# VectorE's order at the seams between Strassen products in a hybrid decoder layer

## The chip, the cores and the metric

The kernel runs on one core of a Trainium2 chip. The metric is the device time of one launch in microseconds (us), the median of the runs shown. A profile is one further execution of the same program.

## The reference

One layer of a decoder trunk is applied to a prompt of 512 tokens and to 8 single-token samples. The large products in it are what the change touches:

```python
h   = modulate(rmsnorm(x, norm1_g), sh1, sc1)
z   = h @ w_in                          # 2048 -> 6144: q, k, v and the RWKV inputs
...                                     # windowed attention and RWKV-7 time mixing on z
x   = x + gt1 * (concat(att, rw) @ w_out)               # 2048 -> 2048
h2  = modulate(rmsnorm(x, norm2_g), sh2, sc2)
gate, up = split(h2 @ w_gu, 2)                          # 2048 -> 2 * 5632
x   = x + gt2 * ((silu(gate) * up) @ w_down)            # 5632 -> 2048
```

## The kernel before

The 520 tokens (528 in the first stage) stand along the free axis, features along the 128 partitions. Every large product is made in pieces of 256 output columns by `product` and `combine`, which carry out one level of Strassen's scheme in the Strassen-Winograd form.

`product` goes over pairs of 128-row blocks of the contraction, numbered i from 0: eight of them in the gate, up, output and input products, five or six in the down products. For two pairs at a time it

- loads the weights into a `raw` tile (L130, one DMA for each pair, issued by SyncE). There are two `raw` buffers (`RAW=2`), each for two pairs;
- makes the three weight sums on VectorE (L143, L144, L145), called *weight steps* below;
- for each pair casts the seven weight blocks to their high part on ScalarE (L149) and subtracts to get the *low part* on VectorE (L150). Both go into an `hl` tile, of which there are three (`HL=3`);
- for each of the seven sums M1, M2, M6, M7, M4, M5, M3, in this order, issues three matmuls into that sum's PSUM bank: high weight by high x, high weight by low x, low weight by high x. So a pair is 21 matmuls, and the third of each three needs the low part.

There is one PSUM bank for each of the seven sums, and the next product uses the same seven. `combine` empties them: ScalarE copies M1 (L163), then VectorE makes seven additions, which read M2 (L164), M6 (L165), M7 (L166), M4 (L167), M5 (L168 and L169) and M3 (L170). A bank can be written by the next product when its reader is done.

Around the products: in the gate-and-up loop (22 rounds `u`, two products `g{u}` and `u{u}` each) ScalarE makes a tanh of the gate result (L1419), VectorE multiplies it in (L1420), and after the up product VectorE multiplies both (L1422) and SyncE stores the result. In the down loop there are four groups of pairs, eight products `d{group}{u}` each; VectorE adds each result to `y` (L1440 twice, L1445, L1446). Before each group, `act_blocks` prepares its x blocks (L118 to L125).

The instructions are written in program order, but `TileContext(nc, schedule_with_timeline_sim=True)` plans the order of every engine's queue: it goes through the program with its own timing model, and of the instructions that are ready there the one that is earlier in the program goes first. On the chip each queue then runs in the planned order, with waits.

Of the kernel before, what the change touches and what calls it, by code (L numbers as in the profile page):

```python
# [17 lines left out]
P = 128  # L18
# [60 lines left out]
def hymba_step(tc, a):  # L79
# [18 lines left out]
    def strassen(mkpool, sfx, ht, NX=8, RAW=2, HL=3, PC=2, PT=1, S4="ps", placed=None):  # L98
        wf, xp, tp, sm_, pt_ = placed or [mkpool(n + sfx) for n in ("wts", "x", "tmp")] + [None, None]
        sm_, pt_, turn_ = sm_ or tp, pt_ or tp, [0]  # L100
        psF, psG = mkpool("ps" + sfx, space=PSUM, side="left"), mkpool("px" + sfx, space=PSUM, side="right")

        def psf(name, tag="ps"):
            return (psG if tag == "ps" else psF).tile([P, 512], F32, tag=tag, name=name, bufs=1)

        def pair_tile(name, tag="pc"):
            return (pt_ if tag == "pt" else tp).tile([P, 2, 2 * ht], F32, tag=tag, name=name, bufs=dict(pc=PC, pt=PT).get(tag, 1))

        def act_blocks(t, name):
# [12 lines left out]
            for o, src in ((0, t[:, 0:1]), (1, t[:, 2:4]), (3, s4)):  # L122
                e = o + src.shape[1]
                ac.copy(x[:, 0, o:e], src)  # L124
                ve.tensor_sub(x[:, 1, o:e], src, x[:, 0, o:e].bitcast(F32))  # L125
            return x

        def columns(src):
            def load(raw, k, name):
                sp.dma_start(raw.rearrange("p (k m) c -> p k (m c)", k=2), src[k * P : (k + 2) * P, :].rearrange("(k p) m -> p k m", p=P))  # L130
            return load

        def product(load, kpairs, xs, name, hook=None):

            M = {m: psf(f"{name}{m}", m) for m in order}
            last = len(xs) - 1
            for i0 in range(0, len(xs), 2):
                nb = min(2, len(xs) - i0)

                tw = wf.tile([P, 2, 8, P], F32, tag="raw", name=f"{name}w{i0}", bufs=RAW)[:, :nb]  # L140
                for j in range(nb):
                    load(tw[:, j, :4], kpairs[i0 + j], f"{name}{i0 + j}")
                ve.tensor_sub(tw[:, :, 4:6], tw[:, :, 1:3], tw[:, :, 0:1].to_broadcast([P, nb, 2, P]))  # L143
                ve.tensor_add(tw[:, :, 6], tw[:, :, 5], tw[:, :, 1])  # L144
                ve.tensor_sub(tw[:, :, 7], tw[:, :, 3], tw[:, :, 6])  # L145
                for j in range(nb):
                    i, x = i0 + j, xs[i0 + j]
                    w = wf.tile([P, 2, 7, P], F32R, tag="hl", name=f"{name}hl{i}", bufs=HL)
                    ac.copy(w[:, 0], tw[:, j, 1:])  # L149
                    ve.tensor_sub(w[:, 1], tw[:, j, 1:], w[:, 0].bitcast(F32))  # L150
                    for m in order:
                        for wi, xi, st_, en_ in ((0, 0, i == 0, False), (0, 1, False, False), (1, 0, False, i == last)):
                            mm(M[m][:, :ht], w[:, wi, wsel[m]], x[:, xi, xsel[m]], start=st_, stop=en_)
                    if hook:
                        hook()
            return M

        def combine(M, name, c=None):
            c = pair_tile(f"c_{name}") if c is None else c
            q = {(i, j): c[:, i, j * ht : (j + 1) * ht] for i in range(2) for j in range(2)}  # L160
            m1_ = q[0, 0]
            v = {m: t[:, :ht] for m, t in M.items()}
            ac.copy(m1_, v["M1"])  # L163
            ve.tensor_add(q[1, 0], m1_, v["M2"])  # L164
            ve.tensor_add(q[1, 1], m1_, v["M6"])  # L165
            ve.tensor_add(q[0, 1], q[1, 1], v["M7"])  # L166
            ve.tensor_sub(q[0, 0], q[0, 1], v["M4"])  # L167
            ve.tensor_add(q[1, 1], q[1, 1], v["M5"])  # L168
            ve.tensor_add(q[0, 1], q[0, 1], v["M5"])  # L169
            ve.tensor_add(q[1, 1], q[1, 1], v["M3"])  # L170
            return c

        return tp, wf, xp, psF, psf, pair_tile, act_blocks, columns, product, combine

    from contextlib import ExitStack

    with ExitStack() as top:
        def pools(stack):
# [85 lines left out]
        NRAW, NRAWF, NLW, NRA = 5, 5, 3, 2  # L264
        AQ = sp
        pha = mid.enter_context(ExitStack())
        tp, wf, xp, psF, psf, pair_tile, act_blocks, columns, product, combine = strassen(lambda name, **kw: pools(pha)(name, **{"side": RIGHT, **kw}), "a", HS, PC=3)

        pp_ = pools(pha)("par")
        omw = pp_.tile([P, 48], F32, name="omw")  # L270
# [558 lines left out]
        with ExitStack() as wk_stack:  # L829
# [501 lines left out]
        tp, wf, xp, psF, psf, pair_tile, act_blocks, columns, product, combine = strassen(  # L1331
            pool, "f", HT, placed=(wts_, xpool, tmp_, sB, pt_), PT=2, S4="pt")
        NRAW = NRAWF
        count = [0]
# [81 lines left out]
        for u in range(FT // 2):  # L1416
            g = combine(product(columns(w_gu[:, u * 256 : (u + 1) * 256]), kp_g, xs, f"g{u}", hook=fill_f(1) if u > 1 else None), f"g{u}")
            th = pair_tile(f"th{u}", "pt")
            ac.activation(th, g, AF.Tanh, scale=0.5)  # L1419
            ve.scalar_tensor_tensor(g, in0=th, scalar=1.0, in1=g, op0=ALU.add, op1=ALU.mult)  # L1420
            v = combine(product(columns(w_gu[:, DFF + u * 256 : DFF + (u + 1) * 256]), kp_g, xs, f"u{u}", hook=fill_f(1)), f"u{u}")
            ve.tensor_mul(v, v, g)  # L1422
            sp.dma_start(actd[u], v)

        groups = [(0, 5), (5, 11), (11, 17), (17, 22)]
        YD = 2
        for gi, (p0, p1) in enumerate(groups):
            xs = []
            for p in range(p0, p1):
                t = pair_tile(f"a{p}", "pt")  # L1430
                sp.dma_start(t, actd[p])
                xs.append(act_blocks(t, f"a{p}"))
            kp = [2 * p for p in range(p0, p1)]
            for u in range(KT // 2):
                c = combine(product(columns(w_down[:, u * 256 : (u + 1) * 256]), kp, xs, f"d{gi}{u}"), f"d{gi}{u}")
                f2 = slice(2 * u, 2 * u + 2)
                for j in range(2):
                    f = 2 * u + j
                    if j < YD:
                        ve.scalar_tensor_tensor(y[:, f, :SEQ], in0=c[:, j, :SEQ], scalar=modT[:, 48 + f, 0:1], in1=y[:, f, :SEQ],  # L1440
                                                op0=ALU.mult, op1=ALU.add)
                    else:
                        ac.mul(c[:, j, :SEQ], c[:, j, :SEQ], modT[:, 48 + f, 0:1])
                        gp.tensor_add(y[:, f, :SEQ], y[:, f, :SEQ], c[:, j, :SEQ])
                ve.tensor_mul(c[:, :, SEQ:], c[:, :, SEQ:], modT[:, 48 + 2 * u : 50 + 2 * u, 1:9])  # L1445
                ve.tensor_add(y[:, f2, SEQ:], y[:, f2, SEQ:], c[:, :, SEQ:])  # L1446
                if gi == len(groups) - 1:
                    ot = pair_tile(f"ot{u}", "pt").rearrange("p a t -> p (a t)")[:, :1024].rearrange("p (b c) -> p b c", b=4)
                    for j in range(2):
                        f = 2 * u + j  # L1450
                        pt = psf(f"pyt{f}")
                        for b in range(4):
                            tr(pt[:, b * 128 : (b + 1) * 128], y[:, f, b * 128 : (b + 1) * 128])
                        ac.copy(ot[:, :, j * 128 : (j + 1) * 128], pt.rearrange("p (b e) -> p b e", b=4))
                    sp.dma_start(a["y_prompt"][0].rearrange("(b p) d -> p b d", p=P)[:, :, u * 256 : (u + 1) * 256], ot)
# [38 lines left out]
```

## Time and profile before

| | |
|---|---|
| median of three runs | 3308.54 us (3308.37 to 3318.48) |
| the profiled execution's own time | 3317.61 us |
| its span, first to last instruction | 3315.8 us |
| TensorE busy | 2895.7 us, 87% |
| VectorE busy | 2486.4 us, 75% |
| ScalarE busy | 1275.8 us, 38% |
| mean granted TensorE clock | 0.915 |

The times of the stages below are from the span's start. Input products run from 221 to 892 us, attention and time mixing to 1471 us, output products to about 1685 us, gate and up to 2715 us, down products to 3306 us. The granted clock is a share of 2.4 GHz; its two levels here are 1 and 0.5. Idle time in square brackets in a row stands before the first instruction of the row, with what ended it.

### The profile page before, as it was taken

How to read it: one execution, taken by the hardware profiler on the slowest of the kernel's cores; microseconds unless marked ns; L12 is line 12 of the kernel's file. 1: busy time of each engine (PE TensorE's matmuls, PEld its weight loads, DVE VectorE, ACT ScalarE, POOL GpSimd, SP SyncE). 2: the span in 40 equal slices, each digit the busy share in tenths (PEclk: the TensorE clock that was granted, in tenths of full speed). 3: DMA queues.
4: the chain of work that ended last, by engine and by line, in shares of the span. 5: the costliest groups of instructions: out<-in, count | busy, mean ns of one | idle time of the engine just before them, and what ended most of it. 6: DMA issues, size and time to landing. Idle time of an engine off the chain costs nothing.

```text
span 3315.8 us, 59346 instructions
## 1 busy us (share of the span) xinstructions
PE 2895.7 (87%) x23474; PEld 2576.9 (78%) x23474; DVE 2486.4 (75%) x4888; ACT 1275.8 (38%) x2047; POOL 203.5 (6%) x216
## 2 busy tenths in 40 slices
PE   6798999789979699868959999999999987888988
PEld 3577888688946466648859999999999987887887
DVE  6866788777757576657787878777777788889886
ACT  3443443333424244543443333333333343334333
POOL 0100111110010221110000000000000000000000
PEclk8889999889968798869979999999999999999989
DMA  8656666544389895443313333333333332323223
GB/s 272 228 179 211 191 209 199 181 134 135 116 258 295 243 256 136 117 121 109 109 38 99 112 109 109 109 109 103 109 103 115 103 131 93 111 88 115 90 96 103
DMA packets 460443, 476.19 MB, mean 144 GB/s; under 512 B 83070, under 2 KB 384083, under 8 KB 460164
## 3 DMA queue, kind: packets, MB, share of 16 engines
q1 hardware_dynamic: 449984, 452.15, 43.7%
q10 hardware_dynamic: 7428, 11.65, 1.1%
q0 software_dynamic: 2752, 8.60, 0.8%
q8 instruction: 184, 3.01, 0.4%
q14 instruction: 95, 0.78, 0.1%
HBM read 409.10 MB, written 68.17 MB: 144 GB/s over the span
## 4 chain that ended last, share of the span: by engine, by line
DVE 21%; PE 19%; DMA 17%; ACT 4%; issue 4%; SPq 2%; POOL 0%; ACTq 0%; DVEq 0%; POOLq 0%
DMA raw_ada<-in_ada_w 1%; SPq L130 1%; DMA K<-in_cache_k 1%; DVE x_a L125 1%; DMA a<-actd 1%; PE pz L90 1%; PE u15M L90 1%; PE g1M L90 1%; PE ada L90 1%; PE u14M L90 1%; PE u10M L90 1%; PE g17M L90 1%; PE u11M L90 1%; PE g6M L90 1%; PE g2M L90 1%
## 5 line engine op out<-in xcount | busy, mean ns | idle before, releaser
L90 PE MATMUL ada<-raw_ada,c_st 128*32 128x512 f32 x448 | 80.9, 760 | 24.4 <-DMA raw_ada<-in_ada_w 23.8
L1266 POOL TENSOR_TENSOR K<-K,qb 128x1024 f32<-128x1024 f32 (+2 forms) x24 | 58.5, 2447 | 125.4 <-DMA K<-in_cache_k 99.9
L1217 ACT ACTIVATE z<-z,mx 128x128 f32<-128x128 f32 (+3 forms) x64 | 35.8, 559 | 74.6 <-DVE mx L1216 37.8
L1066 ACT ACTIVATE Sall<-pch,ppl 64x64 f32<-64x64 f32 x128 | 39.4, 308 | 57.4 <-PE pch L90 52.6
L90 PEld LDWEIGHTS pg<-AR,BK 64*128 64x128 f32 x256 | 41.5, 238 | 23.4 <-DVE GM L925 8.1
L90 PE MATMUL pg<-AR,BK 64*128 64x128 f32 x256 | 50.1, 344 | 10.2 <-DVE GM L925 6.3
L90 PE MATMUL pz<-ak,aq 64*128 64x256 f32 (+3 forms) x128 | 56.0, 565 | 3.4 <-DVE at L1235 2.9
L198 PE MATMUL pzt<-ident,z 128*128 128x128 f32 x160 | 36.6, 334 | 20.2 <-ACT z L1219 15.6
L1213 DVE SCALAR_TENSOR_TENSOR z<-pz,rnq,T 128x128 f32<-128x128 f32 (+3 forms) x64 | 34.6, 543 | 23.9 <-PE pz L90 22.7
L90 PE MATMUL g0M<-x_g,g0hl 128*128 128x260 f32 x168 | 33.7, 369 | 19.4 <-ACT x_g L124 6.4
L198 PEld LDWEIGHTS pzt<-ident,z 128*128 128x128 f32 x160 | 20.6, 162 | 37.6 <-ACT z L1219 18.2
L90 PEld LDWEIGHTS ada<-raw_ada,c_st 128*32 128x32 f32 x448 | 11.0, 120 | 49.8 <-DMA raw_ada<-in_ada_w 37.7
L90 PE MATMUL o0M<-x_m,o0hl 128*128 128x260 f32 x168 | 32.5, 360 | 18.1 <-ACT x_m L124 14.4
L90 PEld LDWEIGHTS g0M<-x_g,g0hl 128*128 128x128 f32 x168 | 30.0, 263 | 23.0 <-ACT x_g L124 7.7
L90 PEld LDWEIGHTS o0M<-x_m,o0hl 128*128 128x128 f32 x168 | 29.0, 254 | 21.8 <-ACT x_m L124 17.0
L1440 DVE SCALAR_TENSOR_TENSOR y<-c_d,modT,y 128x512 f32<-128x512 f32 x64 | 45.7, 748 | 0.0
L925 DVE TENSOR_TENSOR GM<-pg,cst 128x512 f32<-128x512 f32 x32 | 21.9, 685 | 31.3 <-PE pg L90 31.2
L90 PE MATMUL ao<-adr,c_st 128*32 128x256 f32 x384 | 31.7, 402 | 14.5 <-DMA adr<-in_ada_w 11.1
L1267 DVE TENSOR_REDUCE lg<-K 128x16 f32<-128x1024 f32 (+2 forms) x24 | 29.1, 1213 | 20.4 <-POOL K L1266 20.3
L90 PE MATMUL ada<-xb,c_st 128*32 128x512 f32 x128 | 22.0, 765 | 25.2 <-DMA xb<-in_ada_w 19.9
L90 PE MATMUL po<-zt,av 128*64 128x128 f32 x320 | 40.7, 314 | 0.4 <-ACT zt L1229 0.3
L1219 ACT ACTIVATE z<-z,mx 128x128 f32<-128x128 f32 (+3 forms) x64 | 35.5, 560 | 9.6 <-DVE mx L1218 8.9
(2111 smaller groups left out, 9087.8 us busy)
## 6 DMA issues: line engine op xcount, KB each, us to landing
raw_ada<-in_ada_w SPq DMA_DIRECT2D x56, 1024.0 KB
adr<-in_ada_w SPq DMA_DIRECT2D x48, 512.0 KB
xb<-in_ada_w SPq DMA_DIRECT2D x16, 1024.0 KB
actd<-c_u SPq DMA_DIRECT2D x22, 520.0 KB
a<-actd SPq DMA_DIRECT2D x22, 520.0 KB
lsd<-lx SPq DMA_DIRECT2D x12, 520.0 KB
prd<-rkv SPq DMA_DIRECT2D x24, 256.0 KB
K<-in_cache_k SPq DMA_DIRECT2D x16, 384.0 KB
```

What stands on the lines that cost most here:

```text
L90: pe.matmul(out, lhsT=lhsT, rhs=rhs, start=start, stop=stop)
L125: ve.tensor_sub(x[:, 1, o:e], src, x[:, 0, o:e].bitcast(F32))
L130: sp.dma_start(raw.rearrange("p (k m) c -> p k (m c)", k=2), src[k * P : (k + 2) * P, :].rearrange("(k p) m -> p k m", p=P))
L198: pe.transpose(out, in_=in_, identity=ident[:n, 0:n])
L925: ve.tensor_tensor(GM[i][:, :, :, h], pg, gmask.unsqueeze(2).to_broadcast([P, 2, 2, P]), op=ALU.mult)
L1066: ac.activation(S[hb[h], ch + 1, hb[h]], pc_[hb[h], ch, :], AF.Copy, scale=ppl[hb[h], pr, ch : ch + 1])
L1213: ve.scalar_tensor_tensor(z, in0=pzs[h][:, :nk], scalar=rn[:, qi, h : h + 1], in1=Ts[h][:, 384 - 128 * qi :], op0=ALU.mult, op1=ALU.add)
L1217: ac.activation(z, z, AF.Exp, bias=mx[:, 0:1], accum_out=mx[:, 1:2])
L1219: ac.activation(z, z, AF.Copy, scale=mx[:, 2:3])
L1266: OK.tensor_mul(K[:n], K[:n], qb[:n])
L1267: ve.tensor_reduce(lg[:n, i, :], K[:n].rearrange("p (g e) -> p g e", e=E), axis=AX.X, op=ALU.add)
L1440: ve.scalar_tensor_tensor(y[:, f, :SEQ], in0=c[:, j, :SEQ], scalar=modT[:, 48 + f, 0:1], in1=y[:, f, :SEQ], op0=ALU.mult, op1=ALU.add)
```

## The change

Three things change. `combine` remembers its last addition (L170), and the next `product` issues the low parts of its pairs 1 and 2 behind it on VectorE (`issue_after` adds an ordering edge, no semaphore). The gate multiplications (L1420, L1422 and the store behind it) and the additions of the down products are no longer written right behind their `combine`, but inside the next `product`, behind its second pair (i = 1), that is, behind the first two pairs that share a `raw` tile. A branch that was never taken (`YD`) is gone.

```diff
+        held, after = [None], []
+
         def product(load, kpairs, xs, name, hook=None):
+            prev, held[0] = held[0], None
...
                     ac.copy(w[:, 0], tw[:, j, 1:])
-                    ve.tensor_sub(w[:, 1], tw[:, j, 1:], w[:, 0].bitcast(F32))
+
+                    with tc.issue_after(prev) if i in (1, 2) and prev is not None else nullcontext():
+                        ve.tensor_sub(w[:, 1], tw[:, j, 1:], w[:, 0].bitcast(F32))
...
                     if hook:
                         hook()
+                    while i == 1 and after:
+                        after.pop(0)()
             return M
...
-            ve.tensor_add(q[1, 1], q[1, 1], v["M3"])
+            held[0] = ve.tensor_add(q[1, 1], q[1, 1], v["M3"]).ins
...
-            ve.scalar_tensor_tensor(g, in0=th, scalar=1.0, in1=g, op0=ALU.add, op1=ALU.mult)
+            def gate(g=g, th=th):
+                ve.scalar_tensor_tensor(g, in0=th, scalar=1.0, in1=g, op0=ALU.add, op1=ALU.mult)
+            after.append(gate)
...
-            ve.tensor_mul(v, v, g)
-            sp.dma_start(actd[u], v)
+            def gated(u=u, g=g, v=v):
+                ve.tensor_mul(v, v, g)
+                sp.dma_start(actd[u], v)
+            after.append(gated)
+        while after:
+            after.pop(0)()
...
+                def add(gi=gi, u=u, c=c):
+                    f2 = slice(2 * u, 2 * u + 2)
+                    for f in (2 * u, 2 * u + 1):
+                        ve.scalar_tensor_tensor(y[:, f, :SEQ], in0=c[:, f % 2, :SEQ], scalar=modT[:, 48 + f, 0:1], in1=y[:, f, :SEQ],
                                                 op0=ALU.mult, op1=ALU.add)
+                    ve.tensor_mul(c[:, :, SEQ:], c[:, :, SEQ:], modT[:, 48 + 2 * u : 50 + 2 * u, 1:9])
+                    ve.tensor_add(y[:, f2, SEQ:], y[:, f2, SEQ:], c[:, :, SEQ:])
+                    if gi == len(groups) - 1:
...
+                after.append(add)
+        while after:
+            after.pop(0)()
```

In the last group the transposes, copies and output DMA of each finished piece move with the additions.

## Rows read from the trace of the kernel before

**Rows 1.** Busy time by stage: input products, gate and up, down products

```profile
core 0: us, PE busy (x) PEld busy (x) DVE busy (x) ACT busy (x) POOL busy (x), PEclk, DMA share, GB/s
221.00:892.00 671.00, 606.14 (x4704) 559.23 (x4703) 489.24 (x1012) 247.07 (x344) 71.07 (x96) 0.93 0.55 176
...
1802.00:2715.00 913.00, 859.92 (x6892) 838.20 (x6890) 719.43 (x1167) 335.74 (x398) 0.00 (x0) 0.99 0.34 109
2715.00:3306.00 591.00, 508.28 (x3753) 484.07 (x3754) 495.86 (x949) 213.65 (x280) 0.00 (x0) 0.94 0.31 102
```

**Rows 2.** Tiles' matmuls (ns min/median/max, first and last start): u0, u1, d00

```profile
L90 PE MATMUL u0M<-x_g,u0hl x168: 277/282/297, 1757.7 to 1777.7; 128*128 128x260 f32 x168
...
L90 PE MATMUL u1M<-x_g,u1hl x168: 277/282/388, 1802.2 to 1824.1; 128*128 128x260 f32 x168
...
L90 PE MATMUL d00M<-x_a,d00hl x105: 277/285/587, 2715.5 to 2740.2; 128*128 128x260 f32 x105
```

**Rows 3.** Timeline where g5 and u5 meet (start, us, engine, instructions)

```profile
1972.89 1.08 DVE L150 TENSOR_TENSOR g5hl<-g5w,g5hl 128x896 fp32r<-128x896 f32 x1
...
1975.45 2.09 DVE L150 TENSOR_TENSOR u5hl<-u5w,u5hl 128x896 fp32r<-128x896 f32 x2 [1.14 <-ACT u5hl L149]
1976.18 0.38 ACT L163 COPY c_g<-g5M 128x260 f32<-128x260 f32 x1
...
1976.68 1.30 PE L90 MATMUL u5M<-x_g,u5hl 128*128 128x260 f32 x6
1977.60 0.19 PEld L90 LDWEIGHTS u5M<-x_g,u5hl 128*128 128x128 f32 x1 [0.33 <-DVE u5hl L150]
1977.64 0.69 DVE L143 TENSOR_TENSOR u5w<-u5w 128x512 f32<-128x512 f32 x1
1978.25 0.42 DVE L164 TENSOR_TENSOR c_g<-c_g,g5M 128x260 f32<-128x260 f32 x1
1978.59 0.42 DVE L165 TENSOR_TENSOR c_g<-c_g,g5M 128x260 f32<-128x260 f32 x1
1978.72 10.35 PEld L90 LDWEIGHTS u5M<-x_g,u5hl 128*128 128x128 f32 x86 [0.94 <-DVE c_g L164]
...
1981.15 0.69 DVE L143 TENSOR_TENSOR u5w<-u5w 128x512 f32<-128x512 f32 x1 [0.47 <-DMA u5w<-in_w_gu]
...
1982.10 0.42 DVE L170 TENSOR_TENSOR c_g<-c_g,g5M 128x260 f32<-128x260 f32 x1
...
1983.77 1.24 DVE L1420 SCALAR_TENSOR_TENSOR c_g<-th,c_g 128x1040 f32<-128x1040 f32 x1
1984.44 2.86 ACT L149 CAST u5hl<-u5w 128x896 fp32r<-128x896 f32 x3 [0.81 <-PE u5M L90]
...
1985.41 3.17 DVE L150 TENSOR_TENSOR u5hl<-u5w,u5hl 128x896 fp32r<-128x896 f32 x3
```

**Rows 4.** Timelines of other gate-and-up seams: weight-step waits, and a long TensorE wait

```profile
1780.11 0.69 DVE L143 TENSOR_TENSOR g1w<-g1w 128x512 f32<-128x512 f32 x1 [1.58 <-DMA g1w<-in_w_gu]
...
2133.32 3.86 PEld L90 LDWEIGHTS g9M<-x_g,g9hl 128*128 128x128 f32 x19 [2.29 <-DVE c_u L164]
...
2644.65 0.69 DVE L143 TENSOR_TENSOR u20w<-u20w 128x512 f32<-128x512 f32 x1 [0.88 <-DMA u20w<-in_w_gu]
```

**Rows 5.** Windows at the long wait of g9 (columns as in Rows 1)

```profile
2129.90:2135.90 6.00, 3.77 (x20) 3.36 (x19) 4.55 (x11) 0.94 (x1) 0.00 (x0) 0.80 0.31 99
2135.90:2138.90 3.00, 3.00 (x23) 3.00 (x22) 3.00 (x5) 0.00 (x0) 0.00 (x0) 0.83 0.00 0
```

**Rows 6.** Timeline of down product d15 and its seam with d16

```profile
2966.56 2.63 ACT L149 CAST d15hl<-d15w 128x896 fp32r<-128x896 f32 x3 [4.77 <-PE d15M L90]
...
2967.55 7.79 PE L90 MATMUL d15M<-x_a,d15hl 128*128 128x260 f32 x63 [0.35 <-ACT d15hl L149]
...
2976.28 1.09 DVE L150 TENSOR_TENSOR d16hl<-d16w,d16hl 128x896 fp32r<-128x896 f32 x1
...
2977.42 1.74 PEld L90 LDWEIGHTS d16M<-x_a,d16hl 128*128 128x128 f32 x14 [1.04 <-DVE d16hl L150]
```

**Rows 7.** Timeline where output products o3 and o4 meet

```profile
1591.92 6.51 PEld L90 LDWEIGHTS o4M<-x_m,o4hl 128*128 128x128 f32 x51 [0.35 <-DVE o4hl L150]
```

More of the change, by code (lines that the diff above doesn't have):

```diff
@@ L169, in combine @@
             ve.tensor_add(q[0, 1], q[0, 1], v["M5"])
-            ve.tensor_add(q[1, 1], q[1, 1], v["M3"])
+            held[0] = ve.tensor_add(q[1, 1], q[1, 1], v["M3"]).ins
             return c
-        return tp, wf, xp, psF, psf, pair_tile, act_blocks, columns, product, combine
-    from contextlib import ExitStack
+        return tp, wf, xp, psF, psf, pair_tile, act_blocks, columns, product, combine, after
+    from contextlib import ExitStack, nullcontext
     with ExitStack() as top:
@@ L266, in hymba_step @@
         pha = mid.enter_context(ExitStack())
-        tp, wf, xp, psF, psf, pair_tile, act_blocks, columns, product, combine = strassen(lambda name, **kw: pools(pha)(name, **{"side": RIGHT, **kw}), "a", HS, PC=3)
+        tp, wf, xp, psF, psf, pair_tile, act_blocks, columns, product, combine, after = strassen(lambda name, **kw: pools(pha)(name, **{"side": RIGHT, **kw}), "a", HS, PC=3)
         pp_ = pools(pha)("par")
@@ L1330, in hymba_step @@
         xpool = (xA, xA, xB, xB, xC, xC, xC, xD)
-        tp, wf, xp, psF, psf, pair_tile, act_blocks, columns, product, combine = strassen(
+        tp, wf, xp, psF, psf, pair_tile, act_blocks, columns, product, combine, after = strassen(
             pool, "f", HT, placed=(wts_, xpool, tmp_, sB, pt_), PT=2, S4="pt")
@@ L1419, in hymba_step @@
             ac.activation(th, g, AF.Tanh, scale=0.5)
-            ve.scalar_tensor_tensor(g, in0=th, scalar=1.0, in1=g, op0=ALU.add, op1=ALU.mult)
+            def gate(g=g, th=th):
+                ve.scalar_tensor_tensor(g, in0=th, scalar=1.0, in1=g, op0=ALU.add, op1=ALU.mult)
+            after.append(gate)
             v = combine(product(columns(w_gu[:, DFF + u * 256 : DFF + (u + 1) * 256]), kp_g, xs, f"u{u}", hook=fill_f(1)), f"u{u}")
-            ve.tensor_mul(v, v, g)
-            sp.dma_start(actd[u], v)
+            def gated(u=u, g=g, v=v):
[4 more added lines that the diff above has]
+            after.pop(0)()
         groups = [(0, 5), (5, 11), (11, 17), (17, 22)]
-        YD = 2
         for gi, (p0, p1) in enumerate(groups):
@@ L1435, in hymba_step @@
                 c = combine(product(columns(w_down[:, u * 256 : (u + 1) * 256]), kp, xs, f"d{gi}{u}"), f"d{gi}{u}")
[L1436 to L1440, printed above, removed]
-                                                op0=ALU.mult, op1=ALU.add)
-                    else:
-                        ac.mul(c[:, j, :SEQ], c[:, j, :SEQ], modT[:, 48 + f, 0:1])
-                        gp.tensor_add(y[:, f, :SEQ], y[:, f, :SEQ], c[:, j, :SEQ])
@@ L1445, in hymba_step @@
[L1445 to L1455, printed above, removed]
+                def add(gi=gi, u=u, c=c):
+                    f2 = slice(2 * u, 2 * u + 2)
+                    for f in (2 * u, 2 * u + 1):
+                        ve.scalar_tensor_tensor(y[:, f, :SEQ], in0=c[:, f % 2, :SEQ], scalar=modT[:, 48 + f, 0:1], in1=y[:, f, :SEQ],
+                                                op0=ALU.mult, op1=ALU.add)
+                    ve.tensor_mul(c[:, :, SEQ:], c[:, :, SEQ:], modT[:, 48 + 2 * u : 50 + 2 * u, 1:9])
+                    ve.tensor_add(y[:, f2, SEQ:], y[:, f2, SEQ:], c[:, :, SEQ:])
+                    if gi == len(groups) - 1:
+                        ot = pair_tile(f"ot{u}", "pt").rearrange("p a t -> p (a t)")[:, :1024].rearrange("p (b c) -> p b c", b=4)
+                        for j in range(2):
+                            f = 2 * u + j
+                            pt = psf(f"pyt{f}")
+                            for b in range(4):
+                                tr(pt[:, b * 128 : (b + 1) * 128], y[:, f, b * 128 : (b + 1) * 128])
+                            ac.copy(ot[:, :, j * 128 : (j + 1) * 128], pt.rearrange("p (b e) -> p b e", b=4))
+                        sp.dma_start(a["y_prompt"][0].rearrange("(b p) d -> p b d", p=P)[:, :, u * 256 : (u + 1) * 256], ot)
```

## The prediction

> **What bounds the kernel now.** Read the busy time by stage first [rows 1]. In the gate-and-up loop TensorE is busy 860 of 913 us and VectorE 719, so VectorE has room on average. In the down loop they are level, 508 and 496 of 591, so there each VectorE microsecond in the wrong place shows.
>
> Then take the tiles [rows 2]. u0 runs without a stall: 168 matmuls start between 1757.7 and 1777.7 us, 0.120 each, 20.1 for a product. From u1 to the first down product, 41 products take 2715.5 - 1802.2 = 913.3 us, 22.3 each. So 2.2 us a product, some 88 us in all, are above TensorE's pace in this stage.
>
> Where they lie is in the timeline of a seam [rows 3]. u5's six first matmuls belong to M1; then TensorE waits 0.33 us for low part 1 and 0.94 for L164, which empties M2: 1.27 us. L164 could have begun when the copy of M1 ended, at 1976.56. It begins at 1978.25, because VectorE's queue has low part 1 (half of the pair of 2.09 us) and a weight step (L143, for pairs 2 and 3) in front. That step is itself held by a buffer: the load it reads could start only when g5's last low part was done, at 1973.97, and a load takes about 3.6 us (low part 1 ends at 1977.54, the load into its buffer ends the next weight step's wait at 1981.15). So L143 could hardly start before 1977.6. In nine of the 43 gate-and-up seams the step in front of L164 waits 0.5 us or more for its DMA; the first and the last of them are in [rows 4].
>
> A last thing to see in [rows 3]: ScalarE's cast for pair 3 waits for TensorE until 1984.44, since it needs the `hl` buffer of pair 0. That is 5.72 us after M2 began, 48 matmuls, or 54 with the six of M1. Pair 0 has only 21: its M3 waits for L170 (1982.10), and the queue has pairs 1 and 2 ahead of it.
>
> **The change, part by part.** *Low parts 1 and 2 behind L170.* The instructions are the same, so VectorE's sum is unchanged; only waits move. Low part 2 already stands behind L170 in the gate-and-up seams (L170 at 1982.10, the next low part after it). Low part 1 leaves the way of L164: about 1.05 us. By itself this gains nothing where the weight step stays ahead, since that waits for its load until 1977.6. Whether it gains depends on that load.
>
> For the load, follow pair 0's buffer. Before low part 1 is there, TensorE can do at most the 21 matmuls of pair 0 and the 14 of pair 1 that use its high part. So pair 0 must finish by the 35th matmul instead of about the 54th: 19 x 0.120 = 2.3 us earlier. The cast and low part of pair 3 follow, the load of pairs 6 and 7 follows them, g5's last low part follows that, and so does the load that L143 waits for. If a gate multiplication (1.24 us) comes between, 1.1 us of the 2.3 are left. About 1.1 is what L143 needs (1977.64 back to 1976.56). So I take the 1.27 us of TensorE's wait as removed; the other bound is 0.
>
> What is late next: low part 1 itself. Seven additions start 0.34 us apart (L164 and L165 in [rows 3]), 2.4 us; from 1976.6 they end near 1979.0, and low part 1 near 1980.1 instead of 1977.5. Behind it on VectorE wait low part 2 and the gate; and its end frees the `raw` buffer for pairs 4 and 5. That load now lands near 1983.7 instead of 1981.15. Three weight steps (1.4), the cast (0.94) and the low part (1.09) bring pair 4's high part near 1986.0 and its low part near 1987.1. TensorE, with M2 from 1977.3 and 79 matmuls left of pairs 0 to 3, arrives at 1986.8 and wants the low part at 1987.0. So the wait is 0.05 us, or 1.3 if the gate stands in between; I take 0.6, the middle, because the planner decides it. Net gain for a seam: 1.27 - 0.6 = 0.65; 43 seams give 28 us, with ends of 0 and 55.
>
> *The clock.* A long seam costs twice. After the wait of 2.29 us in g9 [rows 4] the granted clock averages 0.80 over 6 us and 0.83 over 3, from its level of 1 to that of 0.5 and back [rows 5]: 0.20 x 6 + 0.17 x 3 = 1.7 us lost. Over the stage the clock is 0.99 of 913 us [rows 1], about 9 us. Shorter seams should take back two thirds: 6 us (0 to 9).
>
> *Down products.* In d15 the casts of pairs 3 to 5 wait for pair 0's buffer until 2966.56, and TensorE idles 0.35 us for them; at the next seam it idles 1.04 us for low part 0, which the change doesn't move [rows 6]. The first goes, as pair 0 ends earlier; ten products have this regular form: 10 x 0.35 = 4 us. The upper bound takes the 1.04 too, 14 us. At the four group starts `act_blocks` makes L170 late, and low part 1 behind it is late with it; I set that against the irregular seams, at nothing, and price it below.
>
> *Output and input products.* o4 waits 0.35 us for low part 1, which stands just before L164 [rows 7]. Seven such seams: 2.5 us. The 24 input products share VectorE with other work (489 of 671 us, [rows 1]); by the nearest row, that of o4, they could win 24 x 0.35 = 8 or, with 0.6 late as above, lose 14. I take 0.
>
> *Gate, product and accumulation moved.* Nothing by themselves: L1420 already runs at 1983.77, behind L170 and a low part, and its reader, L1422, comes a product later. In the down loop the additions stay behind low part 1. The cover is VectorE's room in gate-and-up; without it each L1420 and L1422 would cost up to 1.24 us. The store behind L1422 moves with it in SyncE's queue, past the first loads of the next product and before those of pairs 4 to 7, which wait for buffers anyway. The last piece has no next product and is flushed at once, so the end is unchanged.
>
> The Trainium skill (Perfetto Trace Analysis, Identifying Performance Opportunities) says that a gap which repeats on the engine that ought to be saturated can mean too few buffers for the next tile. By it the seam is a matter of the two `raw` buffers, which this change leaves as they are, and the 28 us would be 0. The trace bears it out for the loads in front of L164, and that is the first rival's case.
>
> **Sum.** 28 + 6 + 4 + 2.5 = 40.5 us. Against the profiled execution's own 3317.6 us that is 3277; its span is 3315.8, with 1.8 around it. The profiled execution lies 9.1 above the median of the runs, 3308.5; I take the same 40.5 from the median: 3268.
>
> **Rivals.**
>
> *The load keeps the seam.* If pair 0's earlier end is eaten up on the way (ScalarE has the tanh, VectorE the gate between), L143 stays in front of L164 until its load lands, and M2 starts when it does now. For it: nine waits of this kind [rows 4]. Against it: the 2.3 us of lead. Then the 28 and the 6 fall away, and 6.5 are left: 3302, no change that can be told. Should VectorE's queue have L144 and L145 in front of L164 as well, in the room that low part 1 left, M2 comes 0.7 later and this ends above 3308.
>
> *Slower: TensorE starves for low part 1.* Between the start of L164 and the end of low part 1 lie 2.4 + 1.05 = 3.45 us; M2 starts 0.47 after L164 [rows 3]. So TensorE must have 3.0 us of other work, 25 matmuls. It has 30 if its queue takes pair 1's high-part matmuls between pair 0's, and 20 if it takes pair 0 first and stops at pair 1's third matmul. The first six matmuls of u5 show pair 1's third one before M2 today, so the planner must re-order. Strict order costs 0.6 us at a seam; if the load keeps L164 as well, nothing is won, and 43 + 31 seams lose 0.6 each: 44 us, 3353, before any clock. It decides from where fewer than 25 matmuls stand in the queue before that third one. Against it: the queue ran 54 matmuls around pair 0, so the plan does interleave.
>
> *Group starts.* In the down loop low part 1 behind a late L170 costs at most one low part, 1.05, and one clock loss of 1.7, at two seams in each of four groups: 22 us, which leaves 3290. Re-planning in the attention stage can move the end by several us either way.
>
> **How the numbers follow.** Forecast, with its smaller and larger forms: 0.52. Group starts or new waits take half of it: 0.12. Load keeps the seam: 0.14. Starving: 0.22. The predicted time is the forecast's, 3268. Its own range is 3220 (55 + 9 + 14 + 2.5 + 8 = 88 us) to 3298. With the rivals the range is 3220 to 3335: it takes in the first rival and the milder half of the second, and leaves out about 2 in 10, most of it above. A measurement tells about 0.3%, 10 us, from no change: faster 0.63 (the forecast and nearly all of the group starts), same 0.14, slower 0.23.
>
> **What would show it.** Right: L164 begins within 0.3 us of M1's copy; TensorE's weight loads wait under 0.4 us for L164; u1 to d00 takes 41 x 21.6; the cast of pair 3 starts about 2 us sooner after the seam; the loads of pairs 4 and 5 start about 2.5 later. Wrong: L143 to L145 all in front of L164; a TensorE wait for the second low part of each product; waits for pair 4's cast of a microsecond; a granted clock below 0.99 in gate-and-up.

## The result, and the profile after

The changed kernel takes 3425.48 us (3408.39 to 3432.08, four runs) beside 3313.51 of the kernel before on the same chip (3308.37 to 3322.96, four runs). The ratio is 1.0325, 95% interval 1.0292 to 1.0359: 112 us slower, where 41 us faster was forecast, and far outside the range.

The profiled execution took 3424.36 us, 106.75 more than that of before. By stage, from the first matmul start of one tile to that of the next: start to the first input product +16.4, input products -7.1, attention and time mixing +20.3, output products +1.2, gate and up +55.9, down +20.1. These add up to 106.8.

Line numbers have moved: load L130, weight steps L146 to L148, cast L152, low part L155, copy of M1 L170, additions L171 to L177, gate L1429.

The windows of after for the stages of [rows 1], input products, gate and up, down (same columns):

```profile
237.90:901.80 663.90, 601.38 (x4705) 555.06 (x4705) 493.42 (x1013) 245.10 (x344) 68.11 (x96) 0.95 0.55 178
1833.00:2802.00 969.00, 885.62 (x6888) 856.81 (x6888) 726.45 (x1168) 334.07 (x399) 0.00 (x0) 0.97 0.32 103
2802.00:3413.00 611.00, 515.30 (x3755) 489.42 (x3756) 497.56 (x949) 213.60 (x280) 0.00 (x0) 0.93 0.30 98
```

Gate and up: TensorE's busy time grows from 859.9 to 885.6 us, and what is not busy from 53.1 to 83.4. The 25.7 more of busy time are not all a lower clock: a wait shows about 0.2 us shorter in the matmul rows than in the weight loads (0.67 and 0.87 for the same wait at 2022.10 below), so a part of each wait counts as busy. By the weight loads, whose idle time is summed further down, waiting grows by 39.0 us. The granted clock falls from a mean of 0.9925 to 0.9736 (0.99 and 0.97 in the rows), which is 6.8 us of the stage before and 25.6 after, 18.8 more. So about two thirds of the loss is new waiting and one third the clock. VectorE's busy time hardly moves (719 to 726): nothing was added to its work.

The tiles of [rows 2] after: 41 products now take 2802.2 - 1833.3 = 968.9 us, 23.6 each instead of 22.3.

```profile
L90 PE MATMUL u1M<-x_g,u1hl x168: 277/283/420, 1833.3 to 1856.0; 128*128 128x260 f32 x168
...
L90 PE MATMUL d00M<-x_a,d00hl x105: 277/284/584, 2802.2 to 2827.4; 128*128 128x260 f32 x105
```

The timeline of after where g5 and u5 meet, as [rows 3], and on to the seam with g6:

```profile
2020.15 0.37 ACT L170 COPY c_g<-g5M 128x260 f32<-128x260 f32 x1
2020.57 0.66 PEld L90 LDWEIGHTS u5M<-x_g,u5hl 128*128 128x128 f32 x5 [1.30 <-ACT c_g L170]
2021.02 0.69 DVE L146 TENSOR_TENSOR u5w<-u5w 128x512 f32<-128x512 f32 x1 [0.49 <-DMA u5w<-in_w_gu]
2021.63 0.42 DVE L171 TENSOR_TENSOR c_g<-c_g,g5M 128x260 f32<-128x260 f32 x1
...
2022.10 9.61 PEld L90 LDWEIGHTS u5M<-x_g,u5hl 128*128 128x128 f32 x79 [0.87 <-DVE c_g L171]
2022.10 9.82 PE L90 MATMUL u5M<-x_g,u5hl 128*128 128x260 f32 x79 [0.67 <-DVE c_g L171]
2022.30 0.42 DVE L147 TENSOR_TENSOR u5w<-u5w 128x256 f32<-128x256 f32 x1
...
2024.31 0.41 DVE L177 TENSOR_TENSOR c_g<-c_g,g5M 128x260 f32<-128x260 f32 x1
2024.65 2.08 DVE L155 TENSOR_TENSOR u5hl<-u5w,u5hl 128x896 fp32r<-128x896 f32 x2
...
2025.79 4.00 SPq L130 DMA_DIRECT2D u5w<-in_w_gu  x4
2025.79 0.95 ACT L152 CAST u5hl<-u5w 128x896 fp32r<-128x896 f32 x1
2026.65 1.23 DVE L1429 SCALAR_TENSOR_TENSOR c_g<-th,c_g 128x1040 f32<-128x1040 f32 x1
...
2029.37 0.69 DVE L146 TENSOR_TENSOR u5w<-u5w 128x512 f32<-128x512 f32 x1 [0.49 <-DMA u5w<-in_w_gu]
...
2031.15 1.78 ACT L152 CAST u5hl<-u5w 128x896 fp32r<-128x896 f32 x2 [4.40 <-DVE u5w L148]
2032.14 1.73 PEld L90 LDWEIGHTS u5M<-x_g,u5hl 128*128 128x128 f32 x14 [0.43 <-ACT u5hl L152]
2032.40 0.69 DVE L146 TENSOR_TENSOR u5w<-u5w 128x512 f32<-128x512 f32 x1 [1.42 <-DMA u5w<-in_w_gu]
2033.01 1.08 DVE L155 TENSOR_TENSOR u5hl<-u5w,u5hl 128x896 fp32r<-128x896 f32 x1
...
2034.15 8.45 PEld L90 LDWEIGHTS u5M<-x_g,u5hl 128*128 128x128 f32 x70 [0.28 <-DVE u5hl L155]
...
2044.16 0.69 DVE L146 TENSOR_TENSOR g6w<-g6w 128x512 f32<-128x512 f32 x1 [3.54 <-DMA g6w<-in_w_gu]
2044.77 1.08 DVE L155 TENSOR_TENSOR g6hl<-g6w,g6hl 128x896 fp32r<-128x896 f32 x1
...
2045.91 0.19 PEld L90 LDWEIGHTS g6M<-x_g,g6hl 128*128 128x128 f32 x1 [2.72 <-DVE g6hl L155]
```

Read it along the buffer. The weight step L146, waiting for its load, still stands in front of the first addition L171, so the wait that the change was to remove is still there (0.87 us, 0.94 before). This seam is no exception: in 42 of the 44 gate and up products a weight step is the instruction just ahead of the first addition, before and after; it waits 0.5 us or more for its load in 9 of them before and in 19 after. Low part 1 is the first half of the pair at 2024.65 and ends near 2025.7. At 2025.79 SyncE issues the load of pairs 4 and 5: it had waited for exactly this buffer. The load is there for the weight step at 2029.37, pair 4's cast comes at 2031.15, and TensorE waits for it (0.43), then for its low part (0.28), which stands behind another weight step that waits 1.42 for the next load. The lateness is handed on: at the next seam a weight step waits 3.54 us for its DMA in front of low part 0 of g6, and TensorE waits 2.72 for that.

A view that groups TensorE's weight loads by tile shows the same per product (busy, mean ns of one, then idle in total and by what ended it):

```profile
L90 PEld LDWEIGHTS g3M<-x_g,g3hl 128*128 128x128 f32 x168 | 21.9, 202 | 2.4 <-DVE g3hl L155 1.8 <-ACT c_u L170 0.4 <-DVE c_u L171 0.2
...
L90 PEld LDWEIGHTS u5M<-x_g,u5hl 128*128 128x128 f32 x168 | 20.4, 188 | 2.9 <-ACT c_g L170 1.3 <-DVE c_g L171 0.9 <-ACT u5hl L152 0.4
```

Such a row names only its three largest causes. Summed over the 41 products of each kernel, from u1 to u21, with every wait over 0.15 us counted under its cause:

| weight loads' idle time, by what ended it, us | before | after |
|---|---|---|
| additions of `combine` (VectorE) | 43.3 | 27.5 |
| copy of M1 (ScalarE) | 3.3 | 28.9 |
| casts (ScalarE) | 13.7 | 24.6 |
| low parts (VectorE) | 12.7 | 30.6 |
| all, with the shorter waits | 73.5 | 112.5 |
| products with a mean weight load of 195 ns or more | 4 | 14 |

So 15.8 us of the wait for additions did go, and 54.4 came elsewhere. By place in the product: at the seam, in the first seven weight loads, the waits grow from 57.4 to 80.4 us; for pairs 4 and 5, from the 85th weight load on, they grow from nothing to 29.9; for pairs 6 and 7 they fall from 14.9 to 1.3. The 30.6 for low parts are 24.0 for low part 0 and 6.7 for that of pair 4. For low part 1, which the change moves back, TensorE waited 11.4 us before and not at all after.

188 ns is the median weight load of a product at the full granted clock (u1 before); the longest weight load in g3 after takes 331, and its mean of 202 says that the clock fell for a part of the product, as [rows 5] show after one long wait. After, 14 products have such a mean, before 4.

In the down products the place is the same. The timeline of d15 after, as [rows 6]: at the seam the 1.04 for low part 0 is gone and 0.36 for each of two additions is there instead, but in the middle of the product TensorE waits 1.89 for the cast of pair 4, whose load is waited for at 3060.71. Over the 32 down products the waits for casts and low parts fall from 72.9 to 34.1 us in the first 63 weight loads of a product and grow from 14.2 to 49.4 behind them; those for additions and the copy of M1 grow from 13.3 to 29.1.

```profile
3052.65 1.32 PEld L90 LDWEIGHTS d15M<-x_a,d15hl 128*128 128x128 f32 x10 [0.36 <-DVE c_d L173]
...
3054.32 7.27 PEld L90 LDWEIGHTS d15M<-x_a,d15hl 128*128 128x128 f32 x59 [0.36 <-DVE c_d L176]
...
3060.71 0.69 DVE L146 TENSOR_TENSOR d15w<-d15w 128x512 f32<-128x512 f32 x1 [1.60 <-DMA d15w<-in_w_down]
...
3062.49 1.78 ACT L152 CAST d15hl<-d15w 128x896 fp32r<-128x896 f32 x2 [5.90 <-DVE d15w L148]
...
3063.48 5.11 PEld L90 LDWEIGHTS d15M<-x_a,d15hl 128*128 128x128 f32 x42 [1.89 <-ACT d15hl L152]
```

### The profile page after: what moved, and what is told of

It reads as the page before. It is cut to its first block, busy times and chain, and to the rows that moved or that the text cites. A ratio compares the mean times of both kernels' runs of the same rounds, so it can differ in the third digit from the quotient of the medians.

```text
span 3422.6 us, 59434 instructions
## 1 busy us (share of the span) xinstructions
PE 2959.1 (86%) x23474; PEld 2610.2 (76%) x23474; DVE 2498.4 (73%) x4888; ACT 1274.2 (37%) x2047; POOL 206.0 (6%) x216
## 4 chain that ended last, share of the span: by engine, by line
DVE 25%; DMA 18%; PE 7%; issue 4%; ACT 3%; SPq 1%; DVEq 0%; ACTq 0%; POOLq 0%
SPq L130 1%; DVE x_a L125 1%; DMA a<-actd 1%; DVE y L1456 1%; DMA mix<-mixd 0%; DVE x_g L125 0%; DVE c_g L1429 0%; PE d06M L90 0%; PE d36M L90 0%; PE d04M L90 0%; PE d37M L90 0%; DMA u14w<-in_w_gu 0%; DMA d13w<-in_w_down 0%; DMA d02w<-in_w_down 0%; DMA u6w<-in_w_gu 0%
## 5 line engine op out<-in xcount | busy, mean ns | idle before, releaser
L90 PE MATMUL ada<-raw_ada,c_st 128*32 128x512 f32 x448 | 88.6, 848 | 28.0 <-DMA raw_ada<-in_ada_w 27.5
L90 PE MATMUL pz<-ak,aq 64*128 64x128 f32 (+3 forms) x128 | 63.1, 614 | 1.0 <-DVE z L1220 1.0
L90 PE MATMUL o0M<-x_m,o0hl 128*128 128x260 f32 x168 | 31.3, 346 | 19.2 <-ACT x_m L124 14.4
L90 PE MATMUL ada<-xb,c_st 128*32 128x512 f32 x128 | 23.6, 818 | 26.2 <-DMA xb<-in_ada_w 22.8
L90 PEld LDWEIGHTS g0M<-x_g,g0hl 128*128 128x128 f32 x168 | 27.7, 243 | 23.6 <-ACT x_g L124 8.0
L932 DVE TENSOR_TENSOR GM<-pg,cst 128x512 f32<-128x512 f32 x32 | 21.9, 686 | 30.3 <-PE pg L90 30.1
L90 PEld LDWEIGHTS po<-zt,av 128*64 128x64 f32 x320 | 25.1, 154 | 22.6 <-issue 7.9
L1274 DVE TENSOR_REDUCE lg<-K 128x16 f32<-128x1024 f32 (+2 forms) x24 | 29.1, 1211 | 16.1 <-POOL K L1273 16.1
```

The costliest lines, as they stand in the source:

```text
L90: pe.matmul(out, lhsT=lhsT, rhs=rhs, start=start, stop=stop)
L932: ve.tensor_tensor(GM[i][:, :, :, h], pg, gmask.unsqueeze(2).to_broadcast([P, 2, 2, P]), op=ALU.mult)
L1274: ve.tensor_reduce(lg[:n, i, :], K[:n].rearrange("p (g e) -> p g e", e=E), axis=AX.X, op=ALU.add)
```

## The experiments

Three theories. **A, the held buffer:** low part 1 is the last reader of the `raw` buffer of pairs 0 and 1, so behind L170 it delays the load of pairs 4 and 5 and all that follows. **B, the deferral:** the moved gate, product and accumulation cost the time. **C, the late operand:** TensorE starves for low part 1 itself (a rival of the prediction).

All edits are shown against the kernel that is named. Ratios are to the kernel before on the same chip in the same set of runs, with 95% intervals.

### Which part of the change

*Order only* (the change, with gate, product and accumulation back behind their `combine`):

```diff
-            after.append(gate)
+            gate()
...
-            after.append(gated)
+            gated()
...
-                after.append(add)
+                add()
```

> Low parts 1 and 2 behind L170, but gate, product and accumulation where they were. Theory A (low part 1 behind L170 keeps the raw buffer of pairs 0 and 1, so the load of pairs 4 and 5 comes late): the whole loss stays, 3400 to 3435 us, gate-and-up 23.3 us a product. Theory B (the moved gate and accumulations are late, and their buffers with them): 3300 to 3330.

Measured: 1.0273 (1.0238 to 1.0307), 3404.99 us.

*Deferral only* (the change without the ordering edge):

```diff
-                    with tc.issue_after(prev) if i in (1, 2) and prev is not None else nullcontext():
+                    with tc.issue_after(prev) if False else nullcontext():
```

> Only the gate, product and accumulation moved; low parts as before. Theory A: no change, 3300 to 3330 us. Theory B: 3400 or more.

Measured: 1.0008 (0.9987 to 1.0030), 3317.57 us. B falls: by itself the moved work costs nothing that these runs can tell. Whether it adds to the cost of the order is left open by 1.0273 against 1.0325, whose intervals overlap.

*Low part 1 only* and *low part 2 only* (deferral kept, the edge for one pair; for low part 2 with `i == 2`):

```diff
-                    with tc.issue_after(prev) if i in (1, 2) and prev is not None else nullcontext():
+                    with tc.issue_after(prev) if i == 1 and prev is not None else nullcontext():
```

> As the change, but only low part 1 stands behind L170, low part 2 is free. Theory A: all of the loss, 3400 to 3435 us. Theory C (too much VectorE work between L170 and pair 2, so TensorE waits for low parts): some of the loss goes, 3350 to 3380.

> As the change, but only low part 2 stands behind L170, low part 1 is free. Theory A: no loss, 3295 to 3330 us, since low part 2 stood there in gate-and-up already and the raw buffer is free early again. Theory C: a part of the loss stays, 3350 or more.

Measured: low part 1 alone 1.0397 (1.0366 to 1.0428), 3447.23 us; low part 2 alone 0.9980 (0.9953 to 1.0006), 3313.27 us. The whole loss hangs on low part 1.

### The buffer or the operand

*Hold only.* The kernel before, low part 1 where it was, and a copy of four elements out of the `raw` tile of pairs 0 and 1 behind L170. The copy delays no operand of TensorE, only the release of the buffer:

```diff
                     ve.tensor_sub(w[:, 1], tw[:, j, 1:], w[:, 0].bitcast(F32))
+                    if i == 1 and prev is not None:
+                        mark = wf.tile([P, 4], F32, tag="mark", name=f"{name}mark", bufs=1)
+                        with tc.issue_after(prev):
+                            ve.tensor_copy(mark, tw[:, j, 1, :4])
```

> The kernel before, with one addition: behind the last addition of each combine, VectorE copies four elements a partition out of the next product's raw tile of pairs 0 and 1. Low part 1 stays early; only the raw buffer is held until L170. Theory A (the held buffer is the cause): 3380 to 3430 us, u1 to d00 at 23 us or more a product. Theory C (low part 1 itself comes too late for TensorE): no change, 3300 to 3335.

Measured: 1.0533 (1.0484 to 1.0582), 3505.11 us, worse than the change. Its timeline at the same seam:

```profile
2026.99 0.69 DVE L146 TENSOR_TENSOR u5w<-u5w 128x512 f32<-128x512 f32 x1 [0.63 <-DMA u5w<-in_w_gu]
2027.60 1.08 DVE L153 TENSOR_TENSOR u5hl<-u5w,u5hl 128x896 fp32r<-128x896 f32 x1
...
2028.73 17.90 PEld L90 LDWEIGHTS u5M<-x_g,u5hl 128*128 128x128 f32 x135 [1.68 <-DVE u5hl L153]
...
2031.62 0.16 DVE L157 COPY u5mark<-u5w 128x4 f32<-128x4 f32 x1
...
2035.55 0.69 DVE L146 TENSOR_TENSOR u5w<-u5w 128x512 f32<-128x512 f32 x1 [1.46 <-DMA u5w<-in_w_gu]
```

The copy of 0.16 us ends at 2031.78, and the weight step of pairs 4 and 5 finds its load 3.8 us later. A holds. The run is not quite pure: loads being late everywhere, a weight step that waits for one also comes in front of low part 1 here (2026.99), and TensorE waits 1.68 for it. That is C's wait, but as a consequence of a late load. Over the 41 products it is 40.0 of 153.5 us of idle time; 113.5 are left without it, against 62.1 of the kernel before without its own wait for low part 1.

*One-pair buffers.* The same memory from the output products on, cut into four `raw` buffers of one pair instead of two of two pairs, with weight steps pair by pair. Low part 1 then holds one pair's buffer, and the load of pair 4 goes into that of pair 0. Once on the kernel before, once on the changed kernel (there the order also holds from the output products on alone):

```diff
-                tw = wf.tile([P, 2, 8, P], F32, tag="raw", name=f"{name}w{i0}", bufs=RAW)[:, :nb]
-                for j in range(nb):
-                    load(tw[:, j, :4], kpairs[i0 + j], f"{name}{i0 + j}")
...
+                    for j in range(nb):
+                        t1 = wf.tile([P, 8, P], F32, tag="raw", name=f"{name}w{i0 + j}", bufs=2 * RAW)
+                        load(t1[:, :4], kpairs[i0 + j], f"{name}{i0 + j}")
+                        ve.tensor_sub(t1[:, 4:6], t1[:, 1:3], t1[:, 0:1].to_broadcast([P, 2, P]))
+                        ve.tensor_add(t1[:, 6], t1[:, 5], t1[:, 1])
+                        ve.tensor_sub(t1[:, 7], t1[:, 3], t1[:, 6])
```

> The change from the output products on, with four raw buffers of one pair each in place of two of two pairs (same memory), weight steps pair by pair. Low part 1 now holds the load of pair 5 alone. Theory A: at most 25 us above the next kernel. Theory C: 60 us or more above it.

> The kernel before with the same four raw buffers of one pair from the output products on, as the base for the one before. The weight steps are twice as many at about half the length; estimated from the 0.69 and 0.42 us steps, about 0.2 us more for two pairs, which VectorE's room hides in gate-and-up and not in the down products: 3315 to 3350 us.

Measured: on the changed kernel 0.9896 (0.9865 to 0.9928), 3289.53 us; on the kernel before 0.9826 (0.9786 to 0.9865), 3263.60 us. The second is the fastest kernel of the study. The same order that costs 2.1% with two-pair buffers (the run below) costs 26 us, 0.7 to 0.8%, with one-pair buffers. Low part 1 ends as late there as in the change, in the median 5.9 us after the last matmul of the product before (6.0 in the change), and in the gate and up products TensorE waits for it in neither. So C falls as the main cause. The windows of the kernel before with one-pair buffers, gate-and-up and down:

```profile
1797.00:2687.00 890.00, 856.77 (x6884) 835.95 (x6883) 757.27 (x1652) 338.45 (x395) 0.00 (x0) 0.99 0.37 111
2687.00:3246.00 559.00, 498.55 (x3758) 469.07 (x3757) 506.17 (x1185) 214.34 (x281) 0.00 (x0) 0.98 0.34 108
```

VectorE does more work here (757 us in more and smaller instructions against 719 in [rows 1]), and both stages are still shorter, 890 against 913 and 559 against 591. The seam of g5 and u5 shows why:

```profile
1964.15 14.17 SPq L130 DMA_DIRECT2D u5w<-in_w_gu  x5
...
1966.85 0.37 ACT L174 COPY c_g<-g5M 128x260 f32<-128x260 f32 x1
1966.89 0.42 DVE L145 TENSOR_TENSOR u5w<-u5w 128x256 f32<-128x256 f32 x1 [0.48 <-DMA u5w<-in_w_gu]
...
1968.89 0.42 DVE L175 TENSOR_TENSOR c_g<-c_g,g5M 128x260 f32<-128x260 f32 x1
1969.02 0.19 PEld L90 LDWEIGHTS u5M<-x_g,u5hl 128*128 128x128 f32 x1 [0.18 <-DVE u5hl L161]
```

SyncE issues five loads of one pair each, as the buffers come free one at a time, that of pair 4 some 2 us before the seam. A weight step still waits for its load ahead of the first addition (0.48 at 1966.89), but that wait ends before the copy of M1 does. TensorE waits 0.18 us at this seam, for low part 1, instead of 1.27; over the 41 products its waits for additions are 0.8 us instead of 43.3.

### Where in the program

*From the output products on* and *the first half only*: the edge of the change with `and placed`, and with `and not placed`.

> The change in the output, gate-and-up and down products alone; input and small first products as before. Theory A with the stages read from the two traces: the 76 us of gate-and-up and down stay and the 37 us ahead of the output products go, 3380 to 3400. If the earlier stages' loss was chance of a single trace: 3415 or more.

> The change's order of low parts 1 and 2 in the products of the first half (input and attention stages, and the few before the output products) only; the output, gate-and-up and down products keep the order of before (gate and accumulation still stand behind low part 1, which alone moved nothing). The half from the output products on gave 1.0212 [1.0157, 1.0267], the whole change 1.0325 [1.0292, 1.0359]. If the two halves add up, this one gives 1.007 to 1.017, 3340 to 3375 us. If the first half's share of the whole change is chance of the attention stage or a start that differs from run to run, it gives 1.000 to 1.005.

Measured: from the output products on 1.0212 (1.0157 to 1.0267), 3390.55 us; the first half 1.0073 (1.0050 to 1.0095), 3349.51 us. Multiplied they give 1.0287, a little under the 1.0325 of the whole. In the first half's run the first input product starts at 240.0 us instead of 221.5; it starts at 237.9 to 240.0 in all four profiles with that order in the first half, and at 221.5 to 226.3 in the others. From there to the output products it takes 1256.3 us, before 1250.2. So the first half's loss is mainly in the small products ahead of 221 us. It is not the held buffer there: the run that only holds it, in the first half too, starts the first input product at 222.9. What it is was not followed further.

The attention stage itself varies: in the run from the output products on, all engines have before's instruction order up to 1500 us, and that stage still took 594 us instead of 579 in its profile. Most of the +20.3 of the result's table cannot be put down to the change.

### The forecast's first term by itself

*Weight steps behind the first addition.* The kernel before, from the output products on, with one edge: the weight step of pairs 2 and 3 (L143) behind the first addition (L164). Low part 1 stays early. *Both* adds low part 1 behind the same addition:

```diff
-                ve.tensor_sub(tw[:, :, 4:6], tw[:, :, 1:3], tw[:, :, 0:1].to_broadcast([P, nb, 2, P]))
+                with tc.issue_after(prev) if i0 == 2 and prev is not None else nullcontext():
+                    ve.tensor_sub(tw[:, :, 4:6], tw[:, :, 1:3], tw[:, :, 0:1].to_broadcast([P, nb, 2, P]))
...
-            ve.tensor_add(q[1, 0], m1_, v["M2"])
+            held[0] = ve.tensor_add(q[1, 0], m1_, v["M2"]).ins
```

> The kernel before, with one edit from the output products on: the weight steps of pairs 2 and 3 stand behind the first addition of the combination (L164) in VectorE's queue, so that they and their wait for the load no longer stand in front of it. Low part 1 is where it was, so the raw buffer of pairs 0 and 1 comes free as before. My prediction's first term alone: 1.27 us of TensorE's wait at up to 43 gate-and-up seams goes and nothing else comes late, 3290 to 3310 us with attention's chance, ratio 0.990 to 0.997. If the wait only moves behind L164, into the additions that the next product's M6 and M7 banks wait for, the ratio is 0.998 to 1.003.

> As the run with the weight steps behind the first addition, with low part 1 behind that addition too: it ends some 0.5 to 1.2 us later than before instead of the 4 to 5 us of the change. Theory of the held buffer: the load of pairs 4 and 5 is issued 0.5 to 1.2 us later, inside the slack of the product in part, so the loss is a small part of the change's: ratio 0.995 to 1.010. Theory that any move of low part 1 behind the combination starves TensorE at the seam: 1.015 to 1.03.

Measured: steps alone 0.9916 (0.9885 to 0.9948), 3298.38 us; both 1.0055 (1.0031 to 1.0079), 3343.64 us. The seam of g5 and u5 with the steps alone:

```profile
1964.31 0.38 ACT L167 COPY c_g<-g5M 128x260 f32<-128x260 f32 x1
...
1965.59 0.42 DVE L168 TENSOR_TENSOR c_g<-c_g,g5M 128x260 f32<-128x260 f32 x1
1965.73 13.42 PEld L90 LDWEIGHTS u5M<-x_g,u5hl 128*128 128x128 f32 x109 [0.33 <-DVE u5hl L154]
...
1966.27 0.68 DVE L147 TENSOR_TENSOR u5w<-u5w 128x512 f32<-128x512 f32 x1
```

and with both:

```profile
1993.58 0.42 DVE L170 TENSOR_TENSOR c_g<-c_g,g5M 128x260 f32<-128x260 f32 x1
1993.91 1.08 DVE L155 TENSOR_TENSOR u5hl<-u5w,u5hl 128x896 fp32r<-128x896 f32 x1
1994.91 0.68 DVE L147 TENSOR_TENSOR u5w<-u5w 128x512 f32<-128x512 f32 x1
1995.51 0.42 DVE L171 TENSOR_TENSOR c_g<-c_g,g5M 128x260 f32<-128x260 f32 x1
...
1995.98 1.49 PEld L90 LDWEIGHTS u5M<-x_g,u5hl 128*128 128x128 f32 x12 [0.52 <-DVE c_g L171]
...
1998.85 0.69 DVE L147 TENSOR_TENSOR u5w<-u5w 128x512 f32<-128x512 f32 x1 [0.91 <-DMA u5w<-in_w_gu]
```

With the steps alone the 0.94 us for the first addition is gone and the 0.33 for low part 1 is left. The idle time before weight loads, summed as above, falls from 73.5 to 55.7 us (the part for additions from 43.3 to 7.1), and gate and up, from u1 on, take 898.1 us instead of 913.3. With both, the gain turns into a loss, but not by the buffer in the main: the load of pairs 4 and 5 is 1.3 us later, and the waits for pairs grow by 2.3 us in all over the run with the steps alone (38.2 to 40.5). Low part 1 and the weight step stand between the second and the third addition now, and TensorE waits for the third (0.52): the waits for additions are 30.3 us instead of 7.1. Of the 46 us between the two profiles 21 lie from u1 to d00; 14 lie ahead of the output products, where neither kernel has an edge, and cannot be put down to the edit.

*Weight steps of pair 2 behind the first addition, with one-pair buffers*:

> The kernel before with the four raw buffers of one pair each from the output products on (0.9826 [0.9786, 0.9865]) and the weight steps of pair 2 behind the first addition of the combination. If a late load in front of the first addition still costs TensorE a wait at the seams there, 0.975 to 0.981; if the loads are early enough with one-pair buffers that none stood in front, 0.981 to 0.986.

Measured: 0.9935 (0.9910 to 0.9959), 3303.90 us: outside both expectations, and 1.1% slower than without that edge. In its profile low part 2 moved too, to a median of 6.0 us after the last matmul of the product before, from 2.0; the load into its buffer, that of pair 6, is issued at 7.1 instead of 3.1. The edge could buy nothing at the gate-and-up seams, where TensorE waited 0.8 us for additions in all. But the loss is not there: from g0 to d00 the profile takes 987.3 us instead of 983.6, and the down products take 602.0 instead of 568.4. In them TensorE's waits for additions grow from 31.3 to 49.6 us and for low parts from 19.8 to 34.3, while those for casts fall from 24.4 to 9.8. So a load held back by low part 2 is not shown to be the cause.

### The dose

For each kernel with two-pair buffers, the median over the 41 seams from u1 to the last up product of the time from the last matmul of one product to the start of SyncE's load of pairs 4 and 5 of the next, worked out from the timelines, and the mean product from u1 to d00:

| kernel | load of pairs 4, 5 at, us | product, us | ratio of the whole kernel |
|---|---|---|---|
| steps behind the first addition | 0.7 | 21.9 | 0.9916 |
| deferral only | 0.7 | 22.1 | 1.0008 |
| low part 2 only | 0.7 | 22.1 | 0.9980 |
| before | 0.7 | 22.3 | 1 |
| the change, first half only | 0.7 | 22.3 | 1.0073 |
| steps and low part 1 behind it | 2.1 | 22.4 | 1.0055 |
| the change | 6.0 | 23.6 | 1.0325 |
| order only | 6.0 | 23.6 | 1.0273 |
| the change, from the output products on | 6.1 | 23.7 | 1.0212 |
| hold only | 6.5 | 25.0 | 1.0533 |
| low part 1 only | 6.7 | 24.0 | 1.0397 |

With the load at 0.7 a product takes 21.9 to 22.3 us, with the load at 6.0 to 6.7 it takes 23.6 to 25.0. The row at 2.1 is the run whose loss is mostly the additions' own wait, as said above; so the table does not say from where on a later load begins to cost.

## Why the prediction was wrong

**What bounds the kernel** was read rightly: the seams, with 1.27 us of wait in the row that was quoted, and VectorE's sum of work unchanged.

**The gain of 28 us for the seams** is the step that failed, in two places. First, "about 1.1 is what L143 needs ... so I take the 1.27 us of TensorE's wait as removed". Pair 3's cast did come sooner, as predicted (median 6.0 us after the seam instead of 7.6). But the lead was lost on the way to the next seam: 1.6 us at that cast, 0.6 at the load of pairs 6 and 7 (9.2 us after the seam instead of 9.7), and 0.4 instead of the 1.1 that was needed at the load of pairs 2 and 3, issued 3.3 us before the end of the product instead of 2.9. The step L146 starts 0.6 after it instead of 0.8, and so still stands in front of the first addition. That is the first rival's case. L171 begins 1.1 us after the copy of M1 ends (2020.52 to 2021.63), where 0.3 was to show the forecast right. The gain was to be had otherwise: with the weight step itself behind the addition, 0.9916, or 27.7 us of 3326.05, of which the profiles show 15.2 in gate and up.

Second, "what is late next: low part 1 itself", whose price of 0.05 to 1.3 us was the wait of one product for pair 4. The load was taken 2.5 us later; it came 5.3 later (0.7 to 6.0). Some 1.3 of the missing 2.8 us are the first failure again, since the seven additions start behind the waiting weight step and not at once; another 0.7 is the copy of M1, which starts later itself; the rest are the other weight steps (L147, L148) between the additions. Even so the wait for pairs 4 and 5 comes to 29.9 us, 0.73 a product, near the 0.6 that was taken. What was wrong is that the price ended there. The load of pairs 4 and 5 delays the weight steps, the low parts behind them and the loads that these release, so the next product's first operands are late as well: at g6 a weight step waits 3.54 us for its load in front of low part 0. The seam's waits, which the sum had at nothing, grew from 57.4 to 80.4 us over the 41 products. The low parts have 24.0 of that, where they had 11.4, and the copy of M1 grew by 25.6, as the copy now starts in the median when the product's last matmul ends, not 0.7 us before (in u5 TensorE waits 1.30 for it). The last pair's low part ends 3.4 us before that copy in the median, and TensorE's waits for pairs 6 and 7 are 1.3 us in all, so M1's last matmul seems to stand later in TensorE's queue. Why the plan has it there was not tested.

**The clock** was to give back 6 us. It took 18.8 more, 25.6 instead of 6.8 us of the stage.

**Down products** were to gain 4 us. The wait for low part 0 at d15's seam did go, as the larger bound had it (two waits of 0.36 for additions instead of 1.04), but the casts of pairs 4 and 5 are waited for by 1.89 us in the same product; 20 us lost.

**Output and input products** stay near the estimate (+1.2 and -7.1, to forecasts of -2.5 and 0). The small products ahead of the first input product were left out of the sum altogether; they cost 16.4.

**Gate, product and accumulation** at nothing: right when they are moved alone (1.0008).

**The rivals.** The slower one, TensorE starving for low part 1, had the right sign and a time of 3353, but its cause is not what happened: in the change's own gate-and-up products TensorE never waits for low part 1 (11.4 us before), so the planner did put enough other matmuls ahead. Holding the buffer without moving low part 1 costs more than the change (1.0533), and with one-pair buffers the same late low part costs 0.7 to 0.8%. The first rival had the right step, but its time of 3302 priced nothing for the later load. The rule of the Trainium skill (Perfetto Trace Analysis, Identifying Performance Opportunities), that a repeating gap can mean too little memory for the next tile, by the number of buffers or the size of the tiles, agrees with the runs: buffers that come free one pair at a time, in the same memory, give 0.9826. That the seam could then gain nothing without other buffers does not follow, as the 0.9916 shows.

**Open.** How much of the waits for the copy of M1 (28.9 us) comes from late loads and how much from the new plan of TensorE's queue; why the small products at the start lose 16 to 18 us; how much of attention's +20.3 is chance; and how the loss of the one-pair version of the change (0.7 to 0.8%) divides between low part 1 as an operand and the buffers of pairs 1 and 2 that it and low part 2 still hold.

## What to carry to other kernels

Before an instruction is moved back in a queue, look up whether it is the last reader of a load buffer: then its end is the start of a DMA, and its delay can reach the operands that this load feeds, and the next round's. Price it to the load's landing and on to the next seam, not only to the first consumer. Where a wait in front of the critical instruction comes from another instruction that waits for a load, move that one, or let buffers come free in smaller pieces.

## What the runs showed that was not expected

A copy of 0.16 us a product on an engine with a fifth of its time free in gate and up made the kernel 5.3% slower, only by its place. Cutting two buffers into four of the same total size was worth 1.7%, though VectorE's busy time in gate and up grew by 38 us. And the waits cost more than their length there: 39.0 us more idle time of the weight loads came with 18.8 us more lost to the granted clock.
